# A two-layer hybrid retention/attention trunk: layer 0 opens with two feature blocks over nine column chunks instead of four over fourteen

## The chip, the cores and the metric

The kernel runs on one core of a Trainium2 chip. The metric is device time of one execution in microseconds (us). The kernel before takes 2072.37 us, the median of three runs (2071.63 to 2073.66).

## What is computed

Two layers are applied to x (256 tokens by 2048 features, float32). Only the first part of a layer matters here:

```
c_act = silu(c)
mod = c_act @ w_mod + b_mod
shift, scale, gate = split(mod, 3)
h = rms_norm(x, g_norm) * (1 + scale) + shift
proj = h @ w_in
rq, rk, rv, rg, cq, ckv, kr, mg, bg = split(proj)
...
x = x + gate * out
```

w_mod is 2048 x 6144 and w_in is 2048 x 13376 in each layer. Retention and latent attention follow on the columns of proj, then three more projections; none of that changes.

## The kernel before, in words

All matrices pass through the chip once. A *weight tile* is a load of 512 KB: two feature blocks (of 128 input features) by 512 columns of w_in. Each product is made in split precision: `split_into` (L239 to L242) has ScalarE (ACT) round the tile to its high part and VectorE (DVE) subtract to get the low part, and TensorE (PE) multiplies high by high, high by low and low by high (L274, L277). Raw tiles lie in a pool of five buffers (`WP`), split tiles in a pool of three (`HP`): the split of a tile therefore waits until PE is through with the tile three before it.

`h` must be known before the first product, and h needs scale and shift, which are sums over all 2048 rows of w_mod. So `first_products` (L588) works in *groups* of feature blocks (`GROUPS`, L49). For each group in layer 0, four blocks: it makes h of these blocks, then multiplies them by 14 *column chunks* of 512 columns (28 weight tiles), and meanwhile a background generator, `mod_pair` (L395), fetches scale and shift columns for the next group in 16 loads of 512 KB and has DVE sum the rows: one multiply-and-add (L350) per block of 128 rows, each over 512 columns. The loads go through a ring of two buffers (`RING`): a fetch is issued when the buffer's two rows have been summed. `bg` releases a step of the generator at each weight load, at a rate that `first_products` sets from the number of loads less a `SPARE`. At the end `mod_finish`, `mod_sum` and `make_amul` reduce over the partitions on PE and give `amul` and `mods`; then `make_h` has ACT scale and shift and ACT and DVE split.

The first group's result of a column chunk is copied out of PSUM by ACT (L611); every later group's is added to it by DVE (L613).

The very first group has nothing to run under. `start` (L501) fetches its scale and shift columns into sixteen buffers of their own, computes the mean squares on ACT, transposes x on PE (L525, 32 transposes, copied out by ACT, L527), spreads the reciprocal roots `r` over the partitions (`spread`, L335), sums the scale rows on PE (L535) and the shift rows on DVE (L348, L350), and makes the first h by hand: DVE multiplies by amul (L544), ACT adds the shift (L551), DVE subtracts (L552). In `start` the order of PE, DVE and ACT is the order in which the code is written; from there on a scheduler orders each engine's instructions, weight splits first. All loads are issued by SyncE (SP), in one order.

Of the kernel before, what the change touches and what calls it, by code (L numbers as in the profile page):

```python
# [17 lines left out]
P = 128  # L18
# [27 lines left out]
K_COLS = K_HALF + 2  # L46

TWO_PI = 2.0 * np.pi
GROUPS = ((0, 4), (4, 4), (8, 4), (12, 4)), ((0, 8), (8, 8))  # L49
COLUMNS = 14  # L50
SPARE1 = 3
BRIDGES = 2
SPARE = 8
HP = 3
BIG = 31
WP = 5
# [52 lines left out]
def trunk(ctx: ExitStack, tc: tile.TileContext, x, c, positions, w_mod, b_mod, g_norm, w_in, g_cq,  # L109
# [17 lines left out]
    def aux_tile():  # L127
        return paux.tile([P, 512], F32, name="aux", tag="aux")
# [104 lines left out]
    def load(src, nk, n):  # L233

        t = wp.tile([P, 1024], F32, name="wst", tag="wst")
# [8 lines left out]
    prepared, last_split = [], []  # L244

    def behind_splits():

# [2 lines left out]
    def load_split(src, nk, n, early=False):  # L250
        if prepared and not early:
            return prepared.pop(0)
        bg()
        w = load(src, nk, n)
        t = hp.tile([P, 2, 1024], F32R, name="whl", tag="whl")
        hi = t[:, 0, : nk * n].rearrange("p (k n) -> p k n", k=nk)
        lo = t[:, 1, : nk * n].rearrange("p (k n) -> p k n", k=nk)
        with tc.high_priority(offset=SPLITS):
            last_split.append(split_into(hi, lo, w))
        return hi, lo  # L260
# [131 lines left out]
        DMA.dma_start(w, w_mod[l, k0 * P : (k0 + nd) * P, m0 * P : m0 * P + n].rearrange("(k p) n -> p k n", p=P))  # L392
        return w

    def mod_pair(l, kg, ng):  # L395

        acc = [tmp_tile()[:, : ng * P] for _ in range(2)]
        nd = 8 // ng
        for k0 in range(0, KT, nd):
            for i in range(2):  # L400
                room = ring()
                used[0] += 1
                w = mod_fetch(room[used[0] % len(room)], l, kg + 16 * i, k0, ng)
# [97 lines left out]
    def start():  # L501

        ng = GROUPS[0][0][1]
        nd = 8 // ng
        ws = {(i, k): mod_fetch(quarter("wmod"), 0, 16 * i, k, ng) for i in (1, 0) for k in range(0, KT, nd)}
        ss = small(4).rearrange("p (q t) -> p q t", q=2)
        extra, room = quarter("extra"), quarter("room")
        row, acc = extra[:, : ng * P], extra[:, 512 : 512 + ng * P]
        xh0, hh = blocks("xh0"), Pairs("h")
        with tc.manual_schedule(engines={ENG.PE, ENG.DVE, ENG.Activation}):  # L510
            for q in range(2):
                for t in range(2):
# [7 lines left out]
            for pair in range(KT // 2):  # L520
                ps = aux_tile()
                for a in range(2):
                    for t in range(2):
                        f = (2 * pair + a) * P
                        T.transpose(ps[:, a * S + t * P : a * S + (t + 1) * P],  # L525
                                    xin[t][f // 1024][:, f % 1024 : f % 1024 + P], ident)
                A.activation(xT[:, 2 * pair : 2 * pair + 2, :].rearrange("p a b -> p (a b)"), ps, AF.Copy)  # L527
            r = spread(y, dp.tile([P, S], F32, name="r0", tag="dtab"))
            for k in range(0, ng, 2):
                normalise(xh0[:, k : k + 2, :], k, r)  # L530
            next(rotary, None)
            pr = aux_tile()
            for k0 in range(0, KT, nd):
                for k in range(nd):
                    T.matmul(pr[0:1, : ng * P], cact[:, k0 + k : k0 + k + 1], ws[1, k0][:, k, :], start=k0 + k == 0,  # L535
                             stop=k0 + k == KT - 1)
            for k0 in range(0, KT - nd, nd):
                mod_rows(acc, ws[0, k0], k0, nd)
            A.activation(row[0:1, :], pr[0:1, : ng * P], AF.Copy)
            mod_sum(0, 16, ng, [row[0:1, :]], ones[0:1, 0:1])  # L540
            make_amul(0, 0, ng)
            mod_rows(acc, ws[0, KT - nd], KT - nd, nd)
            for k in range(ng):
                V.tensor_scalar(xh0[:, k, :], xh0[:, k, :], amul[0][:, k : k + 1], None, ALU.mult)  # L544
            first = [w_in[0, k0 * P : (k0 + 2) * P, n : n + 512] for n in (C_RQ, C_RK) for k0 in range(0, ng, 2)]
            prepared.append(load_split(first[0], 2, 512, early=True))
            mod_sum(0, 0, ng, [acc], ones[:, 0:1])
            for k in range(ng):
                hi, lo = hh.block(k)
                shift = mods[0][:, k : k + 1]  # L550
                A.activation(hi, xh0[:, k, :], AF.Identity, bias=shift)  # L551
                V.scalar_tensor_tensor(lo, xh0[:, k, :], shift, hi.bitcast(F32), ALU.add, ALU.subtract)  # L552
            prepared.extend(load_split(src, 2, 512, early=True) for src in first[1:HP])
        return r, hh

    def scaled(l, n):

# [30 lines left out]
    def first_products(l, hh, r, u):  # L588

        dst, groups = Slots(), GROUPS[l]  # L590
        upto = [0] * COLUMNS
# [432 lines left out]
```

## Time and profile before

| | before |
|---|---|
| median of three runs | 2072.37 us |
| the profiled execution | 2073.7 us |
| its span, first to last instruction | 2071.9 us |
| PE busy | 2033.4 us (98%) |
| DVE busy | 1511.5 us (73%) |
| ACT busy | 1062.2 us (51%) |
| mean granted TensorE clock | 0.995 |
| DMA, mean rate | 222 GB/s |

The span lies inside the profiled execution's own time; 1.8 us are around it. A share of busy time is a mean over stages with different limits, so a stage is read from its own stretch of the span. An instruction's line can be that of a helper: L350 is every multiply-and-add of a modulation row, wherever it was called from.

### The profile page before, as it was taken

The numbers are of one execution on the slowest core, as the hardware profiler recorded it, in microseconds if no ns is written. First come the engines' busy times: TensorE is split into PE (matmuls) and PEld (weight loads), VectorE is DVE, ScalarE is ACT, GpSimd is POOL, SyncE is SP. The second block draws the span as 40 slices with busy tenths as digits, with TensorE's granted clock in tenths as the row PEclk, the third lists the DMA queues.
The fourth block names the chain that finished last, engine by engine and source line by source line (L and its number), as shares of the span: only waits on it lengthen the run. The fifth ranks groups of instructions, "written<-read, shape, count | busy, mean of one in ns | idle before, by whom it ended". The sixth has DMA issues, their size and how long they took to land.

```text
span 2071.9 us, 31906 instructions
## 1 busy us (share of the span) xinstructions
PE 2033.4 (98%) x12413; PEld 1806.7 (87%) x12414; DVE 1511.5 (73%) x2258; ACT 1062.2 (51%) x1489; POOL 0.2 (0%) x4
## 2 busy tenths in 40 slices
PE   7999989999999999999999999999999999999998
PEld 4888878898899998888998789889889999988887
DVE  5789977788877777775577776557777778765574
ACT  4554354655456665444454564456544666644453
POOL 0000000000000000000000000000000000000000
PEclk9999999999999999999999999999999999999999
DMA  8988956557866667885569976665677666676572
GB/s 311 315 287 283 299 187 194 155 176 266 304 210 190 182 197 262 275 274 188 184 192 310 308 232 193 193 187 151 201 238 225 199 184 197 206 226 188 191 244 91
DMA packets 263511, 460.60 MB, mean 222 GB/s; under 512 B 18464, under 2 KB 68032, under 8 KB 263360
## 3 DMA queue, kind: packets, MB, share of 16 engines
q1 hardware_dynamic: 263360, 458.57, 69.7%
q8 instruction: 97, 1.59, 0.3%
q14 instruction: 54, 0.44, 0.1%
HBM read 456.41 MB, written 2.10 MB: 221 GB/s over the span
## 4 chain that ended last, share of the span: by engine, by line
PE 85%; DMA 6%; DVE 5%; issue 2%; ACT 2%; SPq 0%; ACTq 0%; DVEq 0%
PE acc L274 51%; PE acc L277 26%; DMA ring<-in_w_mod 5%; DVE whl L242 2%; DVE tmp L350 1%; DMA wmod<-in_w_mod 1%; PE aux L266 1%; PE aux L265 1%; PE aux L264 1%; ACT whl L241 1%; PE acc L265 1%; PE acc L266 1%; PE acc L264 1%; DVE extra L350 0%; PE aux L875 0%
## 5 line engine op out<-in xcount | busy, mean ns | idle before, releaser
L241 ACT ACTIVATE whl<-wst 128x1024 fp32r<-128x1024 f32 (+1 forms) x708 | 708.8, 1007 | 795.0 <-PE acc L277 663.5
L242 DVE TENSOR_TENSOR whl<-wst,whl 128x1024 fp32r<-128x1024 f32 (+1 forms) x708 | 814.5, 1155 | 361.8 <-ACT whl L241 358.2
L274 PE MATMUL acc<-whl,h 128*128 128x512 f32 x2048 | 513.2, 391 | 0.0
L274 PEld LDWEIGHTS acc<-whl,h 128*128 128x128 f32 x2048 | 381.8, 188 | 77.8
L274 PE MATMUL acc<-h,whl 128*128 128x256 f32 x2432 | 330.7, 287 | 10.7 <-ACT h L241 8.0
L274 PEld LDWEIGHTS acc<-h,whl 128*128 128x128 f32 x2432 | 310.0, 194 | 14.3 <-ACT h L241 8.8
L277 PE MATMUL acc<-whl,h 128*128 128x512 f32 x1024 | 281.7, 394 | 2.1 <-DVE whl L242 1.9
L274 PE MATMUL acc<-whl,z 128*128 128x512 f32 x1024 | 255.1, 391 | 1.3 <-ACT whl L241 1.2
L274 PEld LDWEIGHTS acc<-whl,z 128*128 128x128 f32 x1024 | 191.9, 188 | 41.4 <-ACT whl L241 2.0
L277 PEld LDWEIGHTS acc<-whl,h 128*128 128x128 f32 x1024 | 189.8, 188 | 43.0 <-DVE whl L242 5.8
L277 PE MATMUL acc<-h,whl 128*128 128x256 f32 x1216 | 176.3, 286 | 0.0
L277 PEld LDWEIGHTS acc<-h,whl 128*128 128x128 f32 x1216 | 159.7, 194 | 0.1
L350 DVE SCALAR_TENSOR_TENSOR tmp<-ring,cact,tmp 128x512 f32<-128x512 f32 x150 | 111.7, 748 | 48.9 <-DMA ring<-in_w_mod 47.9
L277 PE MATMUL acc<-whl,z 128*128 128x512 f32 x512 | 137.4, 390 | 0.0
L350 DVE SCALAR_TENSOR_TENSOR macc<-wst,cact,macc 128x512 f32<-128x512 f32 x180 | 134.4, 747 | 2.3 <-DMA wst<-in_w_mod 0.2
L277 PEld LDWEIGHTS acc<-whl,z 128*128 128x128 f32 x512 | 95.9, 188 | 19.8
L274 PE MATMUL acc<-c,whl 128*128 128x256 f32 x640 | 102.0, 289 | 0.0
L274 PEld LDWEIGHTS acc<-c,whl 128*128 128x128 f32 x640 | 86.3, 192 | 0.1
L274 PE MATMUL acc<-m,whl 128*128 128x256 f32 x512 | 67.3, 284 | 0.0
L274 PEld LDWEIGHTS acc<-m,whl 128*128 128x128 f32 x512 | 64.0, 192 | 0.1
L274 PE MATMUL acc<-whl,m 128*128 128x512 f32 (+1 forms) x256 | 56.5, 365 | 0.0
L277 PE MATMUL acc<-c,whl 128*128 128x256 f32 x320 | 56.2, 284 | 0.0
(259 smaller groups left out, 1884.9 us busy)
## 6 DMA issues: line engine op xcount, KB each, us to landing
wst<-in_w_in SPq DMA_DIRECT2D x416, 512.0 KB, 4.4
wst<-in_w_mod SPq DMA_DIRECT2D x96, 512.0 KB, 4.7
ring<-in_w_mod SPq DMA_DIRECT2D x80, 512.0 KB, 5.2
wst<-in_w_ret_proj SPq DMA_DIRECT2D x64, 512.0 KB, 5.0
wst<-in_w_mla_proj SPq DMA_DIRECT2D x64, 512.0 KB, 4.5
wst<-in_w_out SPq DMA_DIRECT2D x64, 512.0 KB, 3.7
wst<-in_w_ukv SPq DMA_DIRECT2D x32, 512.0 KB, 4.7
wst<-in_w_uq SPq DMA_DIRECT2D x32, 384.0 KB, 3.9
```

What stands on the lines that cost most here:

```text
L241: A.activation(hi, src, AF.Copy)
L242: return V.tensor_tensor(lo, src, hi.bitcast(F32), ALU.subtract)
L264: T.matmul(o, a[0], b[0], start=start, stop=False, skip_group_check=True)
L265: T.matmul(o, a[0], b[1], start=False, stop=False, skip_group_check=True)
L266: T.matmul(o, a[1], b[0], start=False, stop=stop, skip_group_check=True)
L274: T.matmul(o, x, y, start=start and i == 0, stop=False, skip_group_check=True)
L277: T.matmul(o, x, y, start=False, stop=stop, skip_group_check=True)
L350: V.scalar_tensor_tensor(acc, w[:, k, :], cact[:, k0 + k : k0 + k + 1], acc, ALU.mult, ALU.add)
```

## The change

The first group is cut in two: blocks 0 and 1 over the first nine column chunks (`FIRST`), then blocks 2 and 3 over these nine while the other five take all four blocks. `start` now needs scale and shift of two blocks only: eight loads of 512 KB, each four row blocks by 256 columns; then come three weight tiles, and then eight loads for blocks 2 and 3 with four more weight tiles between them (`later`, `loaded`). Blocks 2 and 3 are summed by `mod_pair` on DVE, scale and shift alike, as 32 rows of 256 columns. In the opening, r is spread right after the first pair of transposes, PE takes scale rows and transposes by turns, and h is made with scale and shift in one step on both ACT and DVE. The last three groups are as before.

```diff
-GROUPS = ((0, 4), (4, 4), (8, 4), (12, 4)), ((0, 8), (8, 8))
+GROUPS = ((0, 2), (2, 2), (4, 4), (8, 4), (12, 4)), ((0, 8), (8, 8))
+FIRST = 9
-SPARE1 = 3
-SPARE = 8
+SPARE = (2, 3, 8, 8, 8), (3, 3)
...
-        w = load(src, nk, n)
+        w = loaded.pop(0) if loaded else load(src, nk, n)
...
-    def mod_pair(l, kg, ng):
+    def mod_pair(l, kg, ng, fetched=None):
...
+                if fetched:
+                    w = fetched[i, k0]
+                else:
+                    used[0] += 1
+                    w = mod_fetch(ring()[used[0] % RING], l, kg + 16 * i, k0, ng)
...
-        ws = {(i, k): mod_fetch(quarter("wmod"), 0, 16 * i, k, ng) for i in (1, 0) for k in range(0, KT, nd)}
+        steps = [(i, k) for k in range(0, KT, nd) for i in (1, 0)]
+        ws = {(i, k): mod_fetch(quarter("wmod") if k else ring()[i], 0, 16 * i, k, ng) for i, k in steps}
+        first = [w_in[0, 0 : 2 * P, n : n + 512]
+                 for n in (C_RQ, C_RK, C_RQ + 512, C_RK + 512, C_RV, C_RV + 512, C_RV + 1024)]
+        loaded.extend(load(src, 2, 512) for src in first[:HP])
+        later = {}
+        for n, (i, k) in enumerate(steps):
+            later[i, k] = mod_fetch(quarter("wmod"), 0, ng + 16 * i, k, ng)
+            if n % 2:
+                loaded.append(load(first[HP + n // 2], 2, 512, quarter("wst") if HP + n // 2 >= WP else None))
...
+            feature_major(0)
             r = spread(y, dp.tile([P, S], F32, name="r0", tag="dtab"))
-            for k in range(0, ng, 2):
-                normalise(xh0[:, k : k + 2, :], k, r)
+            for n, k0 in enumerate(range(0, KT, nd)):
+                mod_rows(acc, ws[0, k0], k0, nd)
+                if n == 0:
+                    normalise(xh0[:, 0:2, :], 0, r)
+                scale_rows(k0)
+                if n < 3:
+                    feature_major(2 * n + 1)
+                    feature_major(2 * n + 2)
             next(rotary, None)
...
+            feature_major(7)
+            prepared.append(load_split(first[0], 2, 512, early=True))
             A.activation(row[0:1, :], pr[0:1, : ng * P], AF.Copy)
+            mod_sum(0, 0, ng, [acc], ones[:, 0:1])
             mod_sum(0, 16, ng, [row[0:1, :]], ones[0:1, 0:1])
             make_amul(0, 0, ng)
...
-                A.activation(hi, xh0[:, k, :], AF.Identity, bias=shift)
-                V.scalar_tensor_tensor(lo, xh0[:, k, :], shift, hi.bitcast(F32), ALU.add, ALU.subtract)
+                A.activation(hi, xh0[:, k, :], AF.Identity, bias=shift, scale=scale)
+                V.tensor_scalar(xh0[:, k, :], xh0[:, k, :], scale, shift, ALU.mult, ALU.add)
+                V.tensor_tensor(lo, xh0[:, k, :], hi.bitcast(F32), ALU.subtract)
...
-            todo = [mod_pair(l, k, 4) for k in range(k1, k1 + n1, 4)]
-            background.extend([lambda m=m: next(m, None) for m in todo for _ in range(17)])
-            rate[0] = len(background) / (sum(kg + ng - k for k in upto) // 2 - (SPARE, SPARE1)[l])
-            for n in range(COLUMNS):
+            if n1 == 2:
+                todo, steps, columns = [second], 9, FIRST
+            else:
+                todo, steps, columns = [mod_pair(l, k, 4) for k in range(k1, k1 + n1, 4)], 17, COLUMNS
+            background.extend([lambda m=m: next(m, None) for m in todo for _ in range(steps)])
+            rate[0] = len(background) / (sum(kg + ng - k for k in upto[:columns]) // 2 - len(prepared) - SPARE[l][i])
+            for n in range(columns):
```

In the changed kernel's numbering the lines named above are L542 (transposes), L544 (their copies), L535 (scale rows), L566 to L568 (h), L630 (ACT's copies out) and L632 (DVE's adds).

How it moves instructions, first on PE in the opening (xin is x, wmod and ring hold rows of w_mod, extra the sums). Before:

```order
L186 MATMUL aux<-cst,rows 128x88
L525 MATMUL aux<-cst,xin 128x128 x32
L335 MATMUL aux<-tmp,ones 128x128 x2
L535 MATMUL aux<-wmod,cact 1x512 x16
L356 MATMUL aux<-ones,extra 128x1 x8
```

Now:

```order
L542 MATMUL aux<-cst,xin 128x128 x4
L335 MATMUL aux<-tmp,ones 128x128 x2
L535 MATMUL aux<-ring,cact 1x256 x4
L542 MATMUL aux<-cst,xin 128x128 x8
L535 MATMUL aux<-wmod,cact 1x256 x4
L542 MATMUL aux<-cst,xin 128x128 x8
L535 MATMUL aux<-wmod,cact 1x256 x4
L542 MATMUL aux<-cst,xin 128x128 x8
L535 MATMUL aux<-wmod,cact 1x256 x4
L542 MATMUL aux<-cst,xin 128x128 x4
L356 MATMUL aux<-ones,extra 128x1 x4
```

Twenty-eight of the 32 transposes now stand behind the spread of r (L335), four by four between sixteen scale matmuls of half the width.

Then on DVE right behind the first h (whl are split weight tiles, tmp the running sums). Before:

```order
L552 SCALAR_TENSOR_TENSOR h<-xh_157,mod_117,h 128x256 x4
L242 TENSOR_TENSOR whl<-wst,whl 128x1024 x5
L348 TENSOR_SCALAR tmp<-ring,cact 128x512 x2
L350 SCALAR_TENSOR_TENSOR tmp<-ring,cact,tmp 128x512 x2
L242 TENSOR_TENSOR whl<-wst,whl 128x1024 x2
L350 SCALAR_TENSOR_TENSOR tmp<-ring,cact,tmp 128x512 x3
```

Now:

```order
L568 TENSOR_TENSOR h<-xh_171,h 128x256
L242 TENSOR_TENSOR whl<-wst,whl 128x1024 x2
L348 TENSOR_SCALAR tmp<-wmod,cact 128x256 x2
L350 SCALAR_TENSOR_TENSOR tmp<-wmod,cact,tmp 128x256 x6
L242 TENSOR_TENSOR whl<-wst,whl 128x1024
L350 SCALAR_TENSOR_TENSOR tmp<-wmod,cact,tmp 128x256 x3
L242 TENSOR_TENSOR whl<-wst,whl 128x1024
L350 SCALAR_TENSOR_TENSOR tmp<-wmod,cact,tmp 128x256 x2
L242 TENSOR_TENSOR whl<-wst,whl 128x1024
L350 SCALAR_TENSOR_TENSOR tmp<-wmod,cact,tmp 128x256 x4
L242 TENSOR_TENSOR whl<-wst,whl 128x1024
```

The rows of blocks 2 and 3 (wmod, 32 in all) now stand ahead of the first row of the ring, between the splits of the first nine tiles.

And on DVE where blocks 2 and 3 are done (part and the narrow mod and amul are the end of their sums), now:

```order
L367 TENSOR_TENSOR part<-tmp,part 128x256
L441 TENSOR_TENSOR tmp<-xT,r_209 128x512
L357 TENSOR_TENSOR mod_117<-aux,vec_88 128x2
L421 SCALAR_TENSOR_TENSOR amul_119<-mod_117,vec_88 128x2
L348 TENSOR_SCALAR tmp<-ring,cact 128x512 x2
L350 SCALAR_TENSOR_TENSOR tmp<-ring,cact,tmp 128x512 x2
L242 TENSOR_TENSOR h<-tmp,h 128x512
L350 SCALAR_TENSOR_TENSOR tmp<-ring,cact,tmp 128x512 x4
L632 TENSOR_TENSOR qk<-qk,acc 128x512 x2
L242 TENSOR_TENSOR whl<-wst,whl 128x1024
```

None of the rows up to L421 and no add (L632) stood before the group of blocks 4 to 7; from that group's first product on, all four engines have the same rows in both kernels.

## Rows read from the trace of the kernel before

**Rows 1.** The page, part 1: busy us, share of the span, instructions.
```profile
PE 2033.4 (98%) x12413; PEld 1806.7 (87%) x12414; DVE 1511.5 (73%) x2258; ACT 1062.2 (51%) x1489; POOL 0.2 (0%) x4
```

**Rows 2.** Timeline, 0 to 75 us: start us, length us, engine, line, operation, [idle before].
```profile
15.84 0.48 DVE L334 TENSOR_SCALAR tmp<-cst,small 128x128 f32<-128x128 f32 x2
...
19.09 13.89 PE L535 MATMUL aux<-wmod,cact 128*1 128x512 f32 x32
...
19.51 0.63 ACT L227 ACTIVATE angle<-angle 128x512 f32<-128x512 f32 x1
...
22.08 0.89 ACT L230 ACTIVATE sin_t<-angle,cst 128x256 f32<-128x256 f32 x2
...
24.30 0.49 DVE L348 TENSOR_SCALAR extra<-wmod,cact 128x512 f32<-128x512 f32 x1 [3.35 <-DMA wmod<-in_w_mod]
...
35.14 1.06 ACT L241 ACTIVATE whl<-wst 128x1024 fp32r<-128x1024 f32 x1 [1.53 <-DMA wst<-in_w_in]
...
39.70 1.68 DVE L552 SCALAR_TENSOR_TENSOR h<-xh,mod,h 128x256 fp32r<-128x256 f32 x4 [0.58 <-ACT h L551]
...
39.72 3.87 PE L274 MATMUL acc<-h,whl 128*128 128x256 f32 x16 [0.87 <-ACT h L551]
...
45.10 2.28 PE L274 MATMUL acc<-h,whl 128*128 128x256 f32 x16
...
53.49 0.48 DVE L348 TENSOR_SCALAR tmp<-ring,cact 128x512 f32<-128x512 f32 x1
```

**Rows 3.** Chain that ended last, 0 to 200 us: start us, us, what.
```profile
142.79 1.92 PE acc L274 x16
...
145.68 1.92 PE acc L274 x16
...
178.50 1.81 PE acc L274 x8
...
181.22 1.81 PE acc L274 x8
```

**Rows 4.** Timeline, 104 to 132 us: the end of the first group.
```profile
103.87 0.75 DVE L350 SCALAR_TENSOR_TENSOR tmp<-ring,cact,tmp 128x512 f32<-128x512 f32 x1 [0.63 <-DMA ring<-in_w_mod]
...
104.54 1.22 DVE L242 TENSOR_TENSOR whl<-wst,whl 128x1024 fp32r<-128x1024 f32 x1
105.67 0.75 DVE L350 SCALAR_TENSOR_TENSOR tmp<-ring,cact,tmp 128x512 f32<-128x512 f32 x1
...
119.71 0.16 DVE L419 SCALAR_TENSOR_TENSOR amul<-mod,vec 128x4 f32<-128x4 f32 x1
...
122.88 0.88 DVE L348 TENSOR_SCALAR tmp<-ring,cact 128x512 f32<-128x512 f32 x2
...
124.14 0.51 PE L274 MATMUL acc<-h,whl 128*128 128x256 f32 x2 [1.47 <-ACT h L241]
```

**Rows 5.** Windows of 2 us: PE, PEld, DVE, ACT, POOL busy, granted clock, DMA.
```profile
284.00:286.00 2.00, 0.00 (x0) 0.00 (x0) 2.00 (x5) 0.06 (x1) 0.00 (x0) 1.00 0.92 333
...
290.00:292.00 2.00, 2.00 (x12) 2.00 (x11) 0.00 (x0) 0.00 (x0) 0.00 (x0) 0.50 0.08 27
```

**Rows 6.** PE's groups by shape, whole span: transposes; busy us, mean ns | idle before.
```profile
L902 PE MATMUL aux<-cst,tmp 128*128 128x128 f32 x64 | 9.6, 272 | 0.0
...
L525 PE MATMUL aux<-cst,xin 128*128 128x128 f32 x32 | 7.3, 413 | 6.6 <-DMA xin<-in_x 4.3 <-ACT xT L527 2.3
```

**Rows 7.** Timeline, 186 to 212 us: the end of the second group.
```profile
188.77 1.27 DVE L613 TENSOR_TENSOR rg<-rg,acc 128x512 f32<-128x512 f32 x2
...
198.42 0.16 DVE L419 SCALAR_TENSOR_TENSOR amul<-mod,vec 128x4 f32<-128x4 f32 x1
```

**Rows 8.** The ring's tile: its fetches, from issue to landing.
```profile
DMA to landing us min/median/max: 3.8/5.2/7.1
```

**Rows 9.** Groups by shape, 40 to 126 us: busy us, mean ns | idle before, releaser.
```profile
L242 DVE TENSOR_TENSOR whl<-wst,whl 128x1024 fp32r<-128x1024 f32 x30 | 36.4, 1220 | 7.9 <-ACT whl L241 7.9
...
L350 DVE SCALAR_TENSOR_TENSOR tmp<-ring,cact,tmp 128x512 f32<-128x512 f32 x32 | 23.7, 749 | 12.5 <-DMA ring<-in_w_mod 12.2
```

More of the change, by code (lines that the diff above doesn't have):

```diff
@@ L230, in rotary_tables, with load @@
             A.activation(sin_t[:, n], a[:, n * S : (n + 1) * S], AF.Sin, scale=cst[:, K_INV + 2 + n : K_INV + 3 + n])
-    def load(src, nk, n):
-        t = wp.tile([P, 1024], F32, name="wst", tag="wst")
+    def load(src, nk, n, t=None):
+        t = wp.tile([P, 1024], F32, name="wst", tag="wst") if t is None else t
         v = t[:, : nk * n].rearrange("p (k n) -> p k n", k=nk)
@@ L242, in split_into @@
         return V.tensor_tensor(lo, src, hi.bitcast(F32), ALU.subtract)
-    prepared, last_split = [], []
+    prepared, loaded, last_split = [], [], []
     def behind_splits():
@@ L400, in mod_pair @@
             for i in range(2):
-                room = ring()
-                used[0] += 1
-                w = mod_fetch(room[used[0] % len(room)], l, kg + 16 * i, k0, ng)
+                if fetched:
[3 more added lines that the diff above has]
+                    w = mod_fetch(ring()[used[0] % RING], l, kg + 16 * i, k0, ng)
                 with behind_splits():
@@ L519, in start, with scale_rows, feature_major @@
             y = rsqrt_small(v, 2)
-            for pair in range(KT // 2):
+            pr = aux_tile()
+            def scale_rows(k0):
+                for k in range(k0, k0 + nd):
+                    T.matmul(pr[0:1, : ng * P], cact[:, k : k + 1], ws[1, k0][:, k - k0, :], start=k == 0, stop=k == KT - 1)
+            def feature_major(pair):
                 ps = aux_tile()
@@ L527, in start @@
                 A.activation(xT[:, 2 * pair : 2 * pair + 2, :].rearrange("p a b -> p (a b)"), ps, AF.Copy)
+            feature_major(0)
             r = spread(y, dp.tile([P, S], F32, name="r0", tag="dtab"))
-            for k in range(0, ng, 2):
-                normalise(xh0[:, k : k + 2, :], k, r)
-            next(rotary, None)
[L532 to L536, printed above, removed]
@@ L537, in start @@
-            for k0 in range(0, KT - nd, nd):
-                mod_rows(acc, ws[0, k0], k0, nd)
+            for n, k0 in enumerate(range(0, KT, nd)):
[6 more added lines that the diff above has]
+                    feature_major(2 * n + 2)
+            next(rotary, None)
+            feature_major(7)
+            prepared.append(load_split(first[0], 2, 512, early=True))
@@ L539, in start @@
             A.activation(row[0:1, :], pr[0:1, : ng * P], AF.Copy)
+            mod_sum(0, 0, ng, [acc], ones[:, 0:1])
             mod_sum(0, 16, ng, [row[0:1, :]], ones[0:1, 0:1])
             make_amul(0, 0, ng)
[L542 to L545, printed above, removed]
@@ L546, in start @@
-            prepared.append(load_split(first[0], 2, 512, early=True))
-            mod_sum(0, 0, ng, [acc], ones[:, 0:1])
             for k in range(ng):
                 hi, lo = hh.block(k)
-                shift = mods[0][:, k : k + 1]
-                A.activation(hi, xh0[:, k, :], AF.Identity, bias=shift)
-                V.scalar_tensor_tensor(lo, xh0[:, k, :], shift, hi.bitcast(F32), ALU.add, ALU.subtract)
+                scale, shift = amul[0][:, k : k + 1], mods[0][:, k : k + 1]
+                A.activation(hi, xh0[:, k, :], AF.Identity, bias=shift, scale=scale)
@@ L553, in start @@
+                V.tensor_scalar(xh0[:, k, :], xh0[:, k, :], scale, shift, ALU.mult, ALU.add)
+                V.tensor_tensor(lo, xh0[:, k, :], hi.bitcast(F32), ALU.subtract)
             prepared.extend(load_split(src, 2, 512, early=True) for src in first[1:HP])
-        return r, hh
+        return r, hh, mod_pair(0, ng, ng, later)
     def scaled(l, n):
@@ L586, in bridge, with first_products @@
             V.tensor_scalar(d, d, add[:, 2 * j : 2 * j + 1], None, ALU.add)
-    def first_products(l, hh, r, u):
+    def first_products(l, hh, r, u, second):
         dst, groups = Slots(), GROUPS[l]
@@ L596, in first_products @@
         for i, (kg, ng) in enumerate(groups):
-            if l == 0 and i == 1:
+            if l == 0 and i == 2:
                 vectors(1)
@@ L622, in layer @@
         if l == 0:
-            r, hh = start()
+            r, hh, second = start()
         else:
-            hh = Pairs("h")
-        tiles = first_products(l, hh, r, u)
+            hh, second = Pairs("h"), None
+        tiles = first_products(l, hh, r, u, second)
         zz = Pairs("z")
```

## The prediction

> **What bounds the kernel now.** I read the page's totals first: PE is busy 98% of the span [rows 1], so the whole is a row of products and time is to be had only where PE has nothing to multiply. Then the timeline of the opening: the first product starts at 39.72 us [rows 2], and all that the change can give lies ahead of it. Third, the chain that ended last: a weight tile is 24 products that follow each other without a hole. The high parts of a tile of the first four column chunks take 1.92 and the next tile's start 2.89 us later (142.79 and 145.68); for the other chunks it is 2.72 (178.50 and 181.22) [rows 3]. Last, the ends of the groups, since DVE and not PE sets when the next group's h is there: in the first group amul is there at 119.71 and the next group's first product at 124.14 [rows 4].
>
> From that product on both kernels have the same instructions on every engine. So the prediction is one number: **when the group of blocks 4 to 7 starts**, 124.14 before. A shift of it reaches the end, for DVE runs late in the groups behind it too: PE stood idle at 284 to 286 with DVE busy throughout [rows 5].
>
> **The opening.** The root's chain is not touched, so the spread's DVE instructions end at 16.3 as before (15.84 plus 0.48) and PE's spread about 0.7 later, at 17.0. What changes is what stands behind it on PE: 28 transposes and 16 scale matmuls of 256 columns. The scale matmuls cost 13.89 us at 512 columns [rows 2], half of it now, 6.95. A transpose of the opening costs 7.3 / 32 = 0.23, one in full swing 9.6 / 64 = 0.15, with means of 413 and 272 ns for the same shape [rows 6]: the opening ran slow. Before, the transposes filled the wait for x; now PE does four and stands idle until the spread. At the fast price the rest is 6.95 + 28 x 0.15 = 11.1, to 28.1. I take slow work for about the first five us, because the first tile after the idle opening also took 5.38 (39.72 to 45.10) instead of 2.89 [rows 2, 3], 2.5 us more: 30.6. Then ACT is in the way: it stands with pair 6, whose copy can start 2.4 before PE is through (four scale matmuls, 1.74, and four transposes, 0.6), at 28.2. Behind it come the copy (0.5), the rotary tables that before ran under the scale rows (19.51 to 22.97, 3.46 [rows 2]), the last pair's copy (0.5) and the high part of the first tile (1.06): 33.7. The scale row's copy (0.4, like the 256-wide ACT rows at 0.89 for two) and PE's small sums (0.5) run beside DVE's low part of the first tile, which the code puts ahead of mod and amul (1.2, to 34.9). The three narrow instructions (0.5), ACT's first h (0.5) and 0.3 for hand-overs put the **first product at 36.2**, 3.5 us earlier than now.
>
> The loads are no limit there: the ninth landed at 24.30 and the seventeenth at 35.14, 1.36 us apiece [rows 2], so the eighth, now the last that the opening needs, is there at about 23, and the first weight tile at 24.3.
>
> The Trainium skill, "TensorE: Matmul & The Clock Gate", Part 1, says that the throttled state is the default and that activity releases it. By that the opening's PE work begins slow whatever the granted clock is shown as, and the sum is the one above; by the fast price throughout, the first product comes at 33.6 and the sum ends 2.6 lower. The trace agrees with the page here: 413 against 272 ns [rows 6].
>
> **Blocks 0 and 1.** Nine tiles: four of 2.89 and five of 2.72, 25.2, and 2.5 for the slow start, since PE has stood nearly still again for about five us: PE is through at **63.9**.
>
> DVE meanwhile has new work. The 32 rows for blocks 2 and 3 are 256 wide; four instructions of that kind and width took 1.68 [rows 2], 0.42 each where half of the 512-wide pitch (103.87 to 104.54, 0.67 [rows 4]) would be 0.34. So 32 x 0.42 = 13.4. Eleven splits (tiles 1 to 8 and three ahead) at 1.13 (104.54 to 105.67): 12.4. Four for the lower halves of h, 1.6; the finish with four subtractions, one normalise and the narrow ones, 2.8. Together 30.2, which from 36.2 gives 66.4. The same comes out from PE: the third split ahead needs the buffer of the ninth tile, which is free at 63.9; ACT 1.06 and DVE 1.13 make 66.1. Behind that split stand the last three subtractions, normalise, two mods and amul, with three hand-overs to ACT and PE: about 3.7. So amul for blocks 2 and 3 is there at **70**, and ACT's two scalings and high part (1.7) give the product at 71.7. **PE idles 7.8 us** where it had none before. The scale rows that PE summed for the old first group are DVE's now; nothing covers them, as DVE has no hole until then.
>
> **Blocks 2 and 3.** Nineteen tiles are 4 x 2.89 + 15 x 2.72 = 52.4 of PE's time, and a slow start of 2.5: 126.6 if PE were the limit. DVE has: 2 + 30 ring rows at 0.45 and 0.70 (0.67, or 0.77 where two rows of one sum follow each other), 21.9; 16 splits left and three ahead, 21.5; 18 adds, which these nine columns need because their first half is already in SBUF, at 1.27 for two [rows 7], 11.4; the rest (a half of h, finish, two normalise) 4.9. Sum 59.7. And it waits: a ring fetch takes 5.2 from issue to landing [rows 8] and isn't issued before its buffer is read. Before, the same 16 fetches took from 53.49 to 119.71, 66.2 us, with 12.5 of waiting for the ring and 7.9 for ACT [rows 9]; for the group after it, with 28 adds, from 122.88 to 198.42, 75.5 [rows 4, 7]. These two are the bounds. I take 69, which is 59.7 and some 9 of waiting, nearer the first because it has the same loads and rate and 18 adds that fill only part of the waits. So amul is there at **139**, and with 2.5 for ACT the group of blocks 4 to 7 starts at **141.5**, 17.4 later than 124.14. PE, through with its last tile at about 132, idles again.
>
> **Sum.** -3.5 (first product) + 7.8 (idle before blocks 2 and 3) + 2.5 (slow clock behind it; after an idle stretch the granted clock was 0.50 [rows 5]) + about 10.6 (DVE slower than PE in blocks 2 and 3, and the idle at their end in place of the short one before) = +17.4. The profiled execution's span of 2071.9 becomes 2089.3, its own time of 2073.7 becomes 2091.1. That run was 1.3 above the median of 2072.37, so the forecast of the median is 2089.8, said as **2090**.
>
> Ends of the unknowns. Low: all of PE's opening fast (33.6), no wait on the ring, hand-overs as short as 1.4: 33.6 + 30.2 + 1.4 + 59.7 + 2.5 = 127.4, +3.3. High: first product at 38.5, the long chain of 75.5: 38.5 + 33.8 + 75.5 + 2.5 = 150.3, +26.2. Range **2074 to 2099**.
>
> **Rivals.**
> 1. *DVE's holes take the new work, and PE is the limit: faster.* DVE idled 20.4 us (12.5 + 7.9) in the old first group [rows 9]; the new work is 13.4 + 11.4 + about 2. If it lay in those holes, blocks 0 to 3 would be PE's 77.6 and one slow start of 2.5 from 36.2, the next group would start at about 117, and the time would be 2072.4 - 7 = 2065. The place is the last split ahead and the finish behind it: it decides whether DVE has its 30.2 done within PE's 27.7, and its 59.7 within 52.4. For it: the sums miss by only 2.5 and 7.3. Against: the holes were waits for the ring and for ACT, and those for the ring stay. Chance 0.07.
> 2. *The low end: no change.* DVE without a wait, opening fast: +0 to +4, about 2074. A measurement of this kernel tells about 0.2% (4.1 us) from nothing. Chance 0.08.
> 3. *The long chain.* The 18 adds come between the rows of the ring as they did in the second group, every fetch is issued later, and DVE needs 75.5: +21 to +26, about 2096. For it: each add also frees the accumulators that the next tile needs. Against: 18 adds, not 28. Chance 0.2.
> 4. *The change does not bring the opening forward*, because 1 KB pieces load slower. If each of the first eight loads took half as long again the eighth would land at about 28, still ahead of ACT's end at 33.7. It would cost nothing; I give it no chance of its own.
>
> **How the numbers follow.** The forecast, +5 to +21, has 0.65; rivals 1, 2 and 3 have 0.07, 0.08 and 0.2. Rival 1 and the uppermost part of 3 are left out of the range. Faster by over 0.2%: 0.07. Within: 0.08. Slower: 0.65 + 0.2 = 0.85.
>
> **What would show it.** Right: first product near 36; about 32 rows of 256 columns on DVE between 40 and 66; a hole of 6 to 9 us on PE ending near 72 with granted clock 0.50 behind it; 18 more adds at L632 than there were at L613; DVE above nine tenths from 72 to 139; the first product of blocks 4 to 7 near 141, behind an idle PE; from there on the same rows shifted. Wrong: PE busy without a hole from 40 to 120; the hole there but DVE idle in it; or the shift at that product lost again further down, which would mean that DVE is not late behind 124.

## The result, and the profile after

The changed kernel takes 2088.68 us, the median of four runs (2087.66 to 2091.47), beside 2072.85 for the kernel before on the same chip: a ratio of 1.0078, 95% interval 1.0065 to 1.0091, slower by 15.8 us. The profiled execution took 2088.13 us, with a span of 2086.3.

The page's totals first, against [rows 1]: PE's share falls by a point because the span grew and PE's work did not.

```profile
PE 2029.7 (97%) x12418; PEld 1807.5 (87%) x12418; DVE 1531.0 (73%) x2312; ACT 1065.3 (51%) x1494; POOL 0.2 (0%) x4
```

The timeline of the changed kernel, from the spread to the group of blocks 4 to 7 (start us, length us, engine, line, operation, [idle before]), to be read beside [rows 2, 4]:

```profile
16.23 1.22 PE L335 MATMUL aux<-tmp,ones 128*128 128x128 f32 x4 [5.76 <-DVE tmp L334]
...
17.39 3.57 PE L535 MATMUL aux<-ring,cact 128*1 128x256 f32 x8
...
22.16 1.89 PE L535 MATMUL aux<-wmod,cact 128*1 128x256 f32 x8
...
28.48 0.63 ACT L227 ACTIVATE angle<-angle 128x512 f32<-128x512 f32 x1
...
32.33 1.04 ACT L241 ACTIVATE whl<-wst 128x1024 fp32r<-128x1024 f32 x1
...
34.80 0.16 DVE L421 SCALAR_TENSOR_TENSOR amul<-mod,vec 128x2 f32<-128x2 f32 x1
...
35.64 6.40 PE L274 MATMUL acc<-h,whl 128*128 128x256 f32 x26 [1.36 <-ACT h L566]
...
63.44 0.61 PE L277 MATMUL acc<-whl,h 128*128 128x512 f32 x2
...
65.23 1.23 DVE L242 TENSOR_TENSOR whl<-wst,whl 128x1024 fp32r<-128x1024 f32 x1 [1.06 <-ACT whl L241]
...
69.31 0.16 DVE L421 SCALAR_TENSOR_TENSOR amul<-mod,vec 128x2 f32<-128x2 f32 x1
...
71.38 4.22 PE L274 MATMUL acc<-h,whl 128*128 128x256 f32 x18 [2.46 <-ACT h L241]
...
128.10 1.07 PE L277 MATMUL acc<-whl,h 128*128 128x512 f32 x4
...
130.76 0.74 DVE L350 SCALAR_TENSOR_TENSOR tmp<-ring,cact,tmp 128x512 f32<-128x512 f32 x1
...
136.13 0.16 DVE L421 SCALAR_TENSOR_TENSOR amul<-mod,vec 128x4 f32<-128x4 f32 x1
...
139.71 0.35 PE L186 MATMUL aux<-cst,rows 72*128 72x72 f32 x1 [3.93 <-DMA rows<-in_g_ckv]
...
141.27 3.77 PE L274 MATMUL acc<-h,whl 128*128 128x256 f32 x18 [1.21 <-ACT h L241]
```

Four marks are to be seen: first product at 35.64 (39.72 before), last product of blocks 0 and 1 ending at 64.05, blocks 2 and 3 beginning at 71.38, blocks 4 to 7 at 141.27 (124.14 before). PE stands nearly still twice, from 64.05 to 71.38 and from 129.17 to 141.27.

The windows of the same kernel between these marks (PE, PEld, DVE, ACT, POOL busy, granted clock, DMA share, GB/s), and three of 2 us behind the first hole:

```profile
35.64:64.05 28.41, 28.29 (x157) 25.39 (x157) 26.00 (x47) 19.29 (x29) 0.00 (x0) 0.89 0.92 312
64.05:71.38 7.33, 1.06 (x14) 0.62 (x12) 5.41 (x13) 4.40 (x8) 0.00 (x0) 0.85 0.53 146
71.38:129.17 57.79, 55.62 (x277) 47.19 (x277) 49.97 (x65) 23.77 (x28) 0.00 (x0) 0.96 0.84 269
129.17:141.27 12.10, 1.74 (x25) 1.14 (x24) 8.10 (x15) 5.83 (x11) 0.00 (x0) 0.70 0.69 237
...
72.00:74.00 2.00, 2.00 (x11) 2.00 (x11) 0.19 (x1) 0.00 (x0) 0.00 (x0) 0.50 0.88 249
74.00:76.00 2.00, 2.00 (x11) 2.00 (x11) 0.96 (x2) 0.00 (x0) 0.00 (x0) 0.50 0.72 273
76.00:78.00 2.00, 2.00 (x19) 2.00 (x18) 1.96 (x4) 1.06 (x1) 0.00 (x0) 0.99 0.23 26
```

And of the kernel before, between its two marks:

```profile
39.70:124.14 84.44, 82.39 (x458) 70.77 (x458) 63.18 (x78) 49.21 (x69) 0.00 (x0) 0.97 0.89 298
```

The windows give the whole shift. Before, PE lacks 2.05 us of work between the first product and blocks 4 to 7; now 6.27 in the first hole, 10.36 in the second, 2.29 elsewhere, 18.92 in all. That is 16.9 more idle; it is busy 4.3 longer (86.71 against 82.39; the mean granted clock of the stretch is 0.90 against 0.97, and behind the hole it is 0.50 for four us); and it starts 4.1 earlier: +17.1, which is 141.27 less 124.14. What DVE did between the two holes, by groups and shape from 71.38 to 141.27 (busy us, mean ns | idle before, releaser):

```profile
L242 DVE TENSOR_TENSOR whl<-wst,whl 128x1024 fp32r<-128x1024 f32 x19 | 23.1, 1216 | 0.0
L350 DVE SCALAR_TENSOR_TENSOR tmp<-ring,cact,tmp 128x512 f32<-128x512 f32 x30 | 22.3, 747 | 7.9 <-DMA ring<-in_w_mod 7.5
L632 DVE TENSOR_TENSOR rv<-rv,acc 128x512 f32<-128x512 f32 x8 | 5.3, 677 | 0.0
L632 DVE TENSOR_TENSOR qk<-qk,acc 128x512 f32<-128x512 f32 x8 | 5.1, 681 | 0.0
...
L632 DVE TENSOR_TENSOR rg<-rg,acc 128x512 f32<-128x512 f32 x2 | 1.3, 674 | 0.0
```

Further on the rows are the same and only shifted: the first product of blocks 12 to 15 comes at 305.50 instead of 288.58 (+16.9). From there to the end the two profiled runs take 1780.8 and 1783.3; in the fourteen profiles of this study that stretch takes 1775 to 1783, so the 2.5 us given back there are no more than its scatter.

### The profile page after: what moved, and what is told of

Read it like the earlier page. It is cut to its first block, busy times and chain, and to the rows that moved or that the text cites. A ratio compares the mean times of both kernels' runs of the same rounds, so it can differ in the third digit from the quotient of the medians.

```text
span 2086.3 us, 31989 instructions
## 1 busy us (share of the span) xinstructions
PE 2029.7 (97%) x12418; PEld 1807.5 (87%) x12418; DVE 1531.0 (73%) x2312; ACT 1065.3 (51%) x1494; POOL 0.2 (0%) x4
## 4 chain that ended last, share of the span: by engine, by line
PE 84%; DVE 7%; DMA 6%; issue 2%; ACT 2%; SPq 0%; ACTq 0%; DVEq 0%
PE acc L274 50%; PE acc L277 25%; DMA ring<-in_w_mod 5%; DVE whl L242 3%; DVE tmp L350 2%; PE aux L266 1%; PE aux L265 1%; PE aux L264 1%; ACT whl L241 1%; PE acc L265 1%; PE acc L264 1%; PE acc L266 1%; PE aux L894 0%; DVE rv L632 0%; DVE rg L632 0%
## 5 line engine op out<-in xcount | busy, mean ns | idle before, releaser
L274 PEld LDWEIGHTS acc<-whl,h 128*128 128x128 f32 x2048 | 381.4, 188 | 81.6 <-issue 2.2
L274 PE MATMUL acc<-h,whl 128*128 128x256 f32 x2432 | 334.8, 289 | 12.4 <-ACT h L241 9.6
L274 PEld LDWEIGHTS acc<-h,whl 128*128 128x128 f32 x2432 | 313.7, 196 | 15.8 <-ACT h L241 10.4
L350 DVE SCALAR_TENSOR_TENSOR tmp<-ring,cact,tmp 128x512 f32<-128x512 f32 x150 | 111.6, 747 | 42.3 <-DMA ring<-in_w_mod 41.4
```

Source lines behind the costliest of these rows:

```text
L274: T.matmul(o, x, y, start=start and i == 0, stop=False, skip_group_check=True)
L350: V.scalar_tensor_tensor(acc, w[:, k, :], cact[:, k0 + k : k0 + k + 1], acc, ALU.mult, ALU.add)
```

## The experiments

Two theories at the start. **A**: DVE's sum (splits, ring rows and the 18 new adds) sets blocks 0 to 3, wherever PE waits. **B**: the hole between the two small groups is the loss. A third, **D**, came from the trace: the ring's sixteen fetches with two buffers, begun at 71, set the pace. All measured, with the times in us of the first product, of the first product of blocks 2 and 3, of blocks 4 to 7 and of blocks 12 to 15, the median, and the ratio to the kernel before on the same chip. The medians come from several chips, on which the kernel before took 2072.85 to 2074.47, so rows are compared by their ratios:

| run | first | 2-3 | 4-7 | 12-15 | median | ratio (95%) |
|---|---|---|---|---|---|---|
| before | 39.7 | - | 124.1 | 288.6 | 2072.85 | 1 |
| the change | 35.6 | 71.4 | 141.3 | 305.5 | 2088.68 | 1.0078 (1.0065 to 1.0091) |
| e3_first5 | 35.5 | 66.5 | 140.9 | 306.9 | 2088.46 | 1.0073 (1.0058 to 1.0088) |
| e4_first14 | 35.6 | 81.5 | 151.5 | 315.6 | 2095.03 | 1.0102 (1.0086 to 1.0119) |
| e2_no_adds | 35.7 | 71.4 | 133.2 | 296.5 | 2079.61 | 1.0034 (1.0022 to 1.0046) |
| e1_vec_later | 36.2 | 72.1 | 141.3 | 308.0 | 2089.28 | 1.0076 (1.0058 to 1.0094) |
| e9_rows_early | 35.0 | 70.3 | 139.9 | 306.3 | 2087.17 | 1.0059 (1.0044 to 1.0074) |
| e6_ring4 | 34.8 | 70.0 | 134.6 | 297.6 | 2078.74 | 1.0023 (1.0013 to 1.0032) |
| e10_before_ring4 | 39.7 | - | 122.2 | 283.5 | 2063.13 | 0.9943 (0.9928 to 0.9957) |
| e13_no_adds_ring4 | 36.3 | 72.2 | 132.5 | 296.1 | 2075.74 | 1.0007 (0.9998 to 1.0017) |
| e14_ring4_early | 34.9 | 70.3 | 135.1 | 298.0 | 2075.08 | 1.0001 (0.9992 to 1.0010) |
| e5_open_four | 41.3 | - | 124.5 | 285.8 | 2070.08 | 0.9978 (0.9968 to 0.9989) |
| e12_open_four_ring4 | 41.4 | - | 123.3 | 284.5 | 2066.83 | 0.9960 (0.9947 to 0.9972) |
| e11_adds_on_pool | 35.3 | 70.8 | 142.5 | 305.1 | 2085.69 | 1.0052 (1.0039 to 1.0066) |

The opening alone varies: kernels with the same one have their first product between 34.8 and 36.3.

**The hole against the sum.** Two kernels move PE's hole and the number of adds in opposite directions.

```diff
-FIRST = 9
+FIRST = 5
...
-SPARE = (2, 3, 8, 8, 8), (3, 3)
+SPARE = (0, 3, 8, 8, 8), (3, 3)
...
-                 for n in (C_RQ, C_RK, C_RQ + 512, C_RK + 512, C_RV, C_RV + 512, C_RV + 1024)]
+                 for n in (C_RQ, C_RK, C_RQ + 512, C_RK + 512, C_RV)]
...
-            if n % 2:
+            if n % 2 and HP + n // 2 < FIRST:
```

> FIRST = 5 instead of 9: five column chunks over blocks 0 and 1 alone, so 10 second adds instead of 18; the w_in loads of the two chunks that now come later are dropped from the opening's list. TensorE runs out of work near 52 instead of 64, the first product of blocks 2 and 3 stays within 2 us of 71.4, so the hole between the two groups grows to 17 to 20 us. Theory A (VectorE's sum sets blocks 0 to 3): 8 adds x 0.65 = 5 us less, product of blocks 4 to 7 at 135 to 138, end 2082 to 2085. Rival B (the hole between the two small groups is the loss): product at 150 to 154, end 2098 to 2101.

```diff
-FIRST = 9
+FIRST = 14
...
-SPARE = (2, 3, 8, 8, 8), (3, 3)
+SPARE = (7, 3, 8, 8, 8), (3, 3)
```

> FIRST = 14 instead of 9, w_mod rows spread over the same first tiles as before: all fourteen column chunks over blocks 0 and 1, so 28 second adds instead of 18. TensorE has work until 78 to 81 and no hole between the small groups. Theory A: 10 adds x 0.65 = 6.5 us more on VectorE, product of blocks 4 to 7 at 146 to 149, end 2093 to 2096. Rival B: the hole of 7.3 us goes, product at 133 to 136, end 2080 to 2083.

PE's timeline with five chunks, with its window between the two marks, and then the timeline with fourteen:

```profile
60.32 0.19 PE L356 MATMUL aux<-ones_h,part 128*128 128x1 bf16 x1 [7.37 <-ACT part L366]
...
66.53 4.21 PE L274 MATMUL acc<-h,whl 128*128 128x256 f32 x18 [2.75 <-ACT h L241]
...
140.90 4.57 PE L274 MATMUL acc<-h,whl 128*128 128x256 f32 x18 [3.10 <-ACT h L241]
```

```profile
66.53:131.00 64.47, 64.47 (x328) 55.33 (x329) 52.09 (x63) 31.68 (x41) 0.00 (x0) 0.96 0.84 280
```

```profile
81.52 3.95 PE L274 MATMUL acc<-h,whl 128*128 128x256 f32 x18 [2.90 <-ACT h L241]
...
142.72 0.19 PE L356 MATMUL aux<-ones_h,part 128*128 128x1 bf16 x1 [15.58 <-ACT part L366]
...
151.48 3.72 PE L274 MATMUL acc<-h,whl 128*128 128x256 f32 x18 [2.24 <-ACT h L241]
```

B falls. With five chunks the first hole grows to some 13.6 us (17 to 20 were expected) and nothing is lost; with fourteen only 2.9 of it is left, and the end comes 6 us later, for PE stands still 15.58 in one piece behind the stage instead. But A's sizes miss on both sides. With ten further adds blocks 4 to 7 begin 10.2 later, not 6.5: the stage of blocks 2 and 3 lasts as long as in the change (69.96 against 69.89) and begins 10.1 later, behind fourteen chunks of PE's work. Eight adds fewer and blocks 2 and 3 begun 4.9 earlier gave 0.4, not 5. There PE took over: it was busy without a gap from 66.53 to beyond 131, while DVE was busy 52.09 of these 64.47, since four chunks more had all their products in this stage.

**The adds left out.**

```diff
+                    if l == 0 and kg == 2 and n < FIRST:
+                        continue
```

> Left out: the nine column chunks' second adds (18 instructions of L632 in the stage of blocks 2 and 3), so these tiles keep only what blocks 0 and 1 gave them until blocks 4 to 7; the output is not the reference's. Theory A, VectorE's added work sets the stage: 18 x 0.65 = 11.7 us less on it, the last w_mod row ends at 119 to 122 instead of 131.5, the first product of blocks 4 to 7 starts at 129 to 132 (TensorE's own last tile at 129 is next in line), end near 2078. Rival D, the two ring buffers and their loads set the pace of the w_mod rows: VectorE waits for the ring by some 10 us more, the product starts at 138 to 141, end 2086 to 2089.

Between the two: 8.0 us come back at blocks 4 to 7, of the 17.1 lost there, and 9.1 in the end, of 15.8; 11.7 were taken from DVE. With two buffers the adds are about half of the loss.

**The wait for the second layer's vectors.** In the second hole ACT waits for PE, PE's transpose L186 for four small loads that SP issued late, from 133.7 on. In the kernel before they were issued from 116.5 on, and the transpose followed the last tile without a wait (a timeline):

```profile
122.44 0.23 PE L186 MATMUL aux<-cst,rows 72*128 72x72 f32 x1
```

```diff
-            if l == 0 and i == 2:
+            if l == 0 and i == 3:
                 vectors(1)
```

> The changed kernel with vectors(1) called one group later (at the start of blocks 8 to 11), so that its PE transpose no longer stands between amul and the first product of blocks 4 to 7. If that wait is what lies between amul (136.13) and the product (141.27): amul stays within 0.5 of 136.1, the product starts at 138.2 to 139.0 and the end comes 2 to 3 us earlier (about 2085 to 2086). Rival, the splits and copies of the hand-over need that time anyway: product at 140.5 to 141.3, end unchanged within 1 us.

Inconclusive. From amul to product it now takes 2.9 (138.41 to 141.31) instead of 5.1, as expected; but in the profiled run, the slowest of four from 2085.36 to 2092.30, the last ring fetch landed late (DVE waited 2.11 for it, its second row at 133.15 instead of 130.76), amul came 2.3 later, and neither mark nor median moved. The wait is real; whether moving it gives anything was not shown.

**Rows earlier, and the ring.**

```diff
-SPARE = (2, 3, 8, 8, 8), (3, 3)
+SPARE = (2, 8, 8, 8, 8), (3, 3)
```

> The changed kernel with SPARE = (2, 8, ...) instead of (2, 3, ...): the w_mod rows of blocks 4 to 7 are spread over the first eleven of the nineteen loads of blocks 2 and 3's stage, not the first sixteen; no work added or taken away. Theory A': the loss of that stage is its tail (last tile at 129.2, product at 141.3), because the last rows and their closing chain (4.6 us of L366, L367, L357, L421, then the hand-over) come behind the last tile; with the rows five loads earlier the last row comes before 128, tiles cover the closing chain, product at 133 to 137, end 2080 to 2085. Rival D (ring loads cannot come sooner): VectorE's ring waits grow from 7.5 to over 14 us, last row still at 130 to 132, product at 139 to 142, end unchanged within 1.5 us.

Rival D's side, in the product (139.94) and the time; the last row came at 131.81, no earlier than the 130.76 of the change. Its mechanism is borne out in part only: the ring's waits in this stage grew from 7.5 to 9.6, not to over 14. So the ring itself:

```diff
-RING = 2
+RING = 4
```

> The changed kernel with RING = 4 instead of 2 buffers for the w_mod rows of the later groups. Theory A (VectorE's own work sets blocks 2 and 3): its waits for the ring (7.5 us in this stage) shrink, but the tiles' splits and adds stay; product of blocks 4 to 7 at 137 to 141, end 2084 to 2088. Rival D (the chain of sixteen ring loads, begun at 71 with two buffers, sets it): product at 130 to 135, end 2077 to 2082.

> The kernel before with RING = 4, a control for the ring: VectorE waits 12.2 us for the ring there between 40 and 126 while TensorE has work. Theory A: no gain, product of blocks 4 to 7 at 123 to 124.5, end within 2 us of before. Rival D (the ring holds before too): product at 118 to 122, end 2067 to 2070.

DVE's ring rows over the whole kernel, in the change with two buffers and with four, then in the kernel before with two and with four:

```profile
L350 DVE SCALAR_TENSOR_TENSOR tmp<-ring,cact,tmp 128x512 f32<-128x512 f32 x150 | 111.6, 747 | 42.3 <-DMA ring<-in_w_mod 41.4
L350 DVE SCALAR_TENSOR_TENSOR tmp<-ring,cact,tmp 128x512 f32<-128x512 f32 x150 | 110.2, 747 | 2.1 <-DMA ring<-in_w_mod 1.1
L350 DVE SCALAR_TENSOR_TENSOR tmp<-ring,cact,tmp 128x512 f32<-128x512 f32 x150 | 111.7, 748 | 48.9 <-DMA ring<-in_w_mod 47.9
L350 DVE SCALAR_TENSOR_TENSOR tmp<-ring,cact,tmp 128x512 f32<-128x512 f32 x150 | 110.1, 747 | 4.1 <-DMA ring<-in_w_mod 3.1
```

Both are misses for the numbers that I had put under A; the end of the kernel before (2063.13) lies below D's range as well. With two more buffers blocks 4 to 7 begin 6.7 us earlier in the change, 5.4 of it in the stage of blocks 2 and 3 and 1.3 ahead of it, where the opening varies; either kernel's time falls by 10 to 11. In the kernel before, most of that gain lies behind the change's place (1.9 at blocks 4 to 7, 5.1 at blocks 12 to 15, 10.1 by the spans). So with four buffers in both the change costs 12.4 at blocks 4 to 7 instead of 17.1, but no less in the end: **15.6 us (2078.74 against 2063.13, same chip), as with two.** D is not the cause, only a share of one stage. The kernel before with four buffers is the fastest of all measured.

**Neither adds nor ring waits.**

> Left out: the nine column chunks' second adds (18 instructions of L632 in the stage of blocks 2 and 3); the output is not the reference's. RING = 4 beside it, so that neither the adds nor the ring hold VectorE. To be set against the changed kernel with RING = 4 (product of blocks 4 to 7 at 134.6, end 2078.7). Theory A (VectorE's sum holds that stage; the tail behind the last tile is there because the rows come late): rows end by 116 to 118, the tiles cover the closing chain, product at 124 to 128, end 2066 to 2071. Rival T (the tail of about 10 us stands whatever VectorE has to do, because of where the rows stand in its program): last tile near 124, product at 132 to 135, end 2076 to 2079.

> The changed kernel with RING = 4 and SPARE = (2, 8, ...): rows of blocks 4 to 7 over the first eleven loads of the stage, all adds kept. Against RING = 4 alone (product 134.6, end 2078.7). Theory A with a place for the tail: the sum on VectorE stays, but the closing chain and the hand-over get under the last tiles: product at 128 to 132, end 2072 to 2076. Rival: rows moved forward push the tiles' splits and adds back by as much, TensorE waits in the middle of the stage: product at 133 to 136, end 2077 to 2080.

(The edits are those above, together.) By the product's mark both rivals held (132.50 and 135.13). The ends, 2075.74 and 2075.08, do not side with them as clearly: the one lies 0.3 below its rival's range, the other in A's. Without adds and ring waits the stage is PE's; its window, then DVE and PE at its end in that kernel, a timeline:

```profile
72.19:128.13 55.94, 55.94 (x301) 47.69 (x301) 47.00 (x58) 25.26 (x31) 0.00 (x0) 0.96 0.93 317
```

```profile
110.17 2.19 DVE L350 SCALAR_TENSOR_TENSOR tmp<-ring,cact,tmp 128x512 f32<-128x512 f32 x3
...
117.44 1.23 DVE L242 TENSOR_TENSOR whl<-wst,whl 128x1024 fp32r<-128x1024 f32 x1 [1.10 <-ACT whl L241]
...
121.20 0.69 DVE L367 TENSOR_TENSOR part<-tmp,part 128x512 bf16<-128x512 f32 x1
...
126.21 1.23 DVE L242 TENSOR_TENSOR whl<-wst,whl 128x1024 fp32r<-128x1024 f32 x1 [1.42 <-ACT whl L241]
126.25 0.40 PE L356 MATMUL aux<-ones_h,part 128*128 128x1 bf16 x10
...
127.06 1.07 PE L277 MATMUL acc<-whl,h 128*128 128x512 f32 x4
...
127.55 0.16 DVE L421 SCALAR_TENSOR_TENSOR amul<-mod,vec 128x4 f32<-128x4 f32 x1
...
132.50 4.53 PE L274 MATMUL acc<-h,whl 128*128 128x256 f32 x18 [4.30 <-ACT h L241]
```

The last row is summed at 112.4, yet amul is there only at 127.55, 15 us later where the chain needs under five (in the change: 131.5 to 136.13). Its steps stand between the tiles' splits in DVE's order, and the splits wait for buffers that PE frees, 2.7 us apiece; in PE's order they stand between the tiles' products (the last part is ready at 121.9, its sums on PE, L356, come at 126.25). PE is busy all of the 55.94 us from 72.19 to 128.13, then idles 4.3. So even with DVE unburdened, blocks 4 to 7 begin 10.3 behind the kernel before with four buffers (122.22): PE starts 3.4 earlier, but idles 9.7 more (10.6 in all, 6.3 of it ahead of blocks 2 and 3, against 0.9) and is busy 4.0 longer (85.6 against 81.6). The same eighteen adds that were worth 8.0 at this mark with two buffers are worth 2.1 with four (134.57 to 132.50). With the adds kept and the rows earlier (135.13), DVE is busy all of 80 to 110 and the place of the rows gains nothing at this mark; the wait of PE in the middle, which the rival named, does not show (busy 29.33 of these 30 us); that its ratio is still 1.0001, against 1.0023 with four buffers alone, comes from further on and is not explained. Whether rows earlier help once the adds are gone too was not run.

**The opening alone.**

```diff
-GROUPS = ((0, 2), (2, 2), (4, 4), (8, 4), (12, 4)), ((0, 8), (8, 8))
+GROUPS = ((0, 4), (4, 4), (8, 4), (12, 4)), ((0, 8), (8, 8))
...
-SPARE = (2, 3, 8, 8, 8), (3, 3)
+SPARE = (5, 8, 8, 8), (3, 3)
...
-                if n == 0:
-                    normalise(xh0[:, 0:2, :], 0, r)
+                if n < 2:
+                    normalise(xh0[:, 2 * n : 2 * n + 2, :], 2 * n, r)
...
-        return r, hh, mod_pair(0, ng, ng, later)
+        return r, hh, None
...
```

> The new opening alone over the old groups of layer 0 (blocks 0 to 3, then 4 to 7, ...): r spread early, scale and shift rows loaded and used by turns, transposes between them, h in one step; no second small group, no extra adds, background spread as before. Theory A (the opening itself is a gain, the 18 adds and the second small group lose it): first product at 36.5 to 38.5 instead of 39.7, product of blocks 4 to 7 at 121 to 123.5, end 1 to 3 us below before (about 2070 to 2072). Rival (the opening came forward only because the first group's loads were halved; with 8 MB of rows their landing and the slow early TensorE hold it): first product at 39 to 41, product of blocks 4 to 7 at 123.5 to 126, end within 1.5 us of before or above it.

> The new opening over the old groups (blocks 0 to 3 first), with RING = 4; the candidate to beat both kernels. Against the kernel before with RING = 4 (first product 39.7, product of blocks 4 to 7 at 122.2, end 2063.1). If the gain of the opening alone (4 us in the end, though its first product came at 41.3) is its own and adds to the ring's: end 2057 to 2060. Rival: that gain was the two-buffer ring falling differently; with the ring's waits gone the later first product shows: product of blocks 4 to 7 at 123 to 125, end 2063 to 2066.

PE and ACT in the opening with two buffers, a timeline:

```profile
27.71 8.74 PE L529 MATMUL aux<-wmod,cact 128*1 128x512 f32 x20
36.39 0.66 PE L536 MATMUL aux<-cst,xin 128*128 128x128 f32 x4
...
37.08 0.60 ACT L538 ACTIVATE xT<-aux 128x512 f32<-128x512 f32 x1 [5.26 <-PE aux L536]
...
41.28 0.50 PE L274 MATMUL acc<-h,whl 128*128 128x256 f32 x2 [1.08 <-ACT h L560]
```

The rival held for the mechanism: with four blocks the rearranged opening is 1.6 us *later*, since the rest of the scale matmuls (8.74) now stands ahead of the last transposes, for which ACT waits 5.26. So turns, early spread and one-step h do not by themselves bring the 4.1 us of the change: it takes the halved rows of the first group. Whether those would gain as much in the old order was not run. Yet the time with two buffers was 0.22% below the kernel before, a gain first seen at blocks 12 to 15 (-2.8); with four buffers all three products are about 1 us or more behind e10 (122.22 and 283.48 against 123.28 and 284.53) and no gain is to be seen (0.9960 against 0.9943, intervals overlapping). That it was the two-buffer ring falling otherwise fits both runs and the waits in the traces (39.7 us for the ring with two buffers, against 47.9 before; 7.0 against 10.9 between the marks of blocks 4 to 7 and 12 to 15, where the gain appears). It was not shown by a run of its own.

**The adds elsewhere.**

```diff
-RING = 2
+RING = 4
...
+                    if spare is not None:
+                        part = spare[:, j * 512 : (j + 1) * 512]
...
+                        A.activation(part, a, AF.Copy)
+                        nc.gpsimd.tensor_tensor(d, d, part, ALU.add)
...
```

> The changed kernel with RING = 4 and the 18 second adds taken off VectorE: ScalarE copies each sum out of PSUM to a spare buffer (18 x 0.6 us; it is busy less than half of that stage) and GpSimd, idle until then, adds it. Theory A: as without the adds, product of blocks 4 to 7 at 124 to 129, end 2066 to 2072. Rival: the adds are slow on GpSimd or slow VectorE beside them (128x512 rows of L350 well above 750 ns), product at 131 to 137, end 2076 to 2082.

The rival, and worse. The window from 78 to 102 us and its groups by shape with the adds on POOL, and the groups of the same stretch with four buffers and the adds on DVE:

```profile
78.00:102.00 24.00, 17.79 (x95) 14.66 (x93) 23.96 (x15) 12.41 (x18) 22.12 (x13) 0.93 0.52 156
```

```profile
L350 DVE SCALAR_TENSOR_TENSOR tmp<-ring,cact,tmp 128x512 f32<-128x512 f32 x9 | 14.4, 1645 | 0.0
...
L242 DVE TENSOR_TENSOR whl<-wst,whl 128x1024 fp32r<-128x1024 f32 x5 | 10.7, 2132 | 6.0 <-ACT whl L241 6.0
```

```profile
L242 DVE TENSOR_TENSOR whl<-wst,whl 128x1024 fp32r<-128x1024 f32 x8 | 9.7, 1218 | 0.0
L350 DVE SCALAR_TENSOR_TENSOR tmp<-ring,cact,tmp 128x512 f32<-128x512 f32 x11 | 8.2, 745 | 0.0
```

Beside POOL a row takes 1645 ns instead of 745 and a split 2132 instead of 1218: each grows by about 0.9 us, more than the 0.65 us that an add cost it, and in these 24 us DVE gets through 14 rows and splits instead of 19, though it has no adds there.

## Why the prediction was right, and where not

**First product, 36.2 forecast, 35.64 measured.** The chain was as written: ACT's tables at 28.48, the first tile's high part ending at 33.4 (forecast 33.7). That ACT and not the loads ends the opening held too; rival 4 stayed without effect. PE's slow start in the opening came too: its first four scale matmuls took 3.57 (at 17.39) and the next four 1.89 (at 22.16), though the recorded granted clock is 1.00 for both. The e5 run adds what the text had not separated: with the rows of four blocks the same rearrangement comes 1.6 later than before, so the gain needs the halved rows.

**First hole, 7.8 forecast, 7.33 measured.** PE was through at 64.05 (63.9), the third split ahead waited for the ninth tile's buffer and came at 65.23, amul at 69.31 (70), the product at 71.38 (71.7). The narrow rows cost 0.42 apiece, as forecast (four in 1.67; the 0.48 that the profile gives as the length of one overlaps its neighbour).

**Slow start behind it, 2.5 forecast.** The granted clock is 0.50 (1.2 GHz) from 72 to 76 and 0.99 (2.4 GHz) in the window from 76 on, with PE busy throughout and nearly idle before. The next tile starts 5.28 behind the first (71.38 to 76.66) instead of 2.89: 2.4 us lost. The clock is 0.50 again from 140 to 144, behind the second hole, where the kernel before had 1.00 (122 to 128); the forecast did not have this, and it does not show at blocks 12 to 15 (+16.9).

**Blocks 2 and 3, 69 forecast from amul to amul, 66.8 measured (69.31 to 136.13).** The 18 adds took 11.7 (11.4), the ring's waits 7.5 (9). Behind amul the forecast had 2.5 and the trace has 5.1, with the transpose L186 waiting for its loads: a wait that the text did not name. The two misses cancel, 141.27 against 141.5: that the mark came out to 0.2 us is luck.

**The step that failed is the reason given for the 10.6 us**, "DVE slower than PE in blocks 2 and 3", with DVE above nine tenths from 72 to 139. DVE was busy 56.3 of these 67 us, 84%, and PE was through at 129.17, not 132. A queue of 59.7 us plus 9 of waiting gave the right sum, but not a sum that falls with each instruction taken away: eight adds fewer gave 0.4, eighteen fewer gave 8.0, and with the ring's waits gone as well only 8.8 in all. DVE's work, the two-buffer ring, and PE's tiles, with the closing chain behind their splits and products, lie a few us apart, so relief of one meets the next.

**The rivals.** Rival 1 (PE as the limit) failed by the first hole, as argued; the e13 run shows that even with DVE unburdened blocks 4 to 7 would not come at 117. Rival 2 is out with 15.8 us. Rival 3's 75.5 us, from the first ring row to amul, did not come: 66.7 with 18 adds (69.39 to 136.13), and 70.8 with 28 (78.25 to 149.05).

**The shift to the end.** +16.9 at blocks 12 to 15 as said, +14.4 between the profiled spans, +15.8 between the medians; +17.4 was forecast.

## What to carry to other kernels

A first stage cut in half can bring its product forward, since the opening has less to load and sum (4.1 us here), but the second half comes due while the first is still being multiplied: count the second closing chain, hand-over and slow start, and every extra add, against it before anything else. Where three limits of a stage lie within a few us, price a relief by a run that takes it away, since a sum of busy times overstates it (here eighteen adds, 11.7 us of DVE, were worth 8.0 or 2.1). Look beside the planned change for the plain wait in the same rows: 48 us of ring waits were in the profile of before, and two more buffers were worth 11.

## What the hardware showed that was not expected

VectorE's two-input instructions took far longer beside GpSimd's elementwise adds: with POOL busy 22.12 of the 24 us from 78 to 102, DVE's row took 1645 ns instead of 745. The Trainium skill, "SBUF — State Buffer", section "Who interferes with whom", says that the two engines share a port pair as an exclusive lock, and that a VectorE instruction with two inputs in SBUF contends there with a GpSimd instruction that reads SBUF, so that the one that comes second stands still instead of both slowing a little. That rows and splits both grow by about 0.9 us (1645 from 745, 2132 from 1218), whatever their length, agrees.
